# A decoder trunk in split float32: gate/up and key/value products by one level of Strassen

## The chip, the cores and the metric

The kernel runs on one core of one Trainium2 chip. The metric is the device time of one execution in microseconds, as the median of several runs. The kernel before takes 2006.05 us (three runs, 2004.75 to 2006.26).

The core's engines work side by side, each through its own instructions in order: TensorE (PE) multiplies, VectorE (DVE) and ScalarE (ACT) work on elements, GpSimd (POOL) adds and issues some transfers, SyncE (SP) issues most transfers. PE writes to PSUM, which has eight banks of 128 partitions x 512 float32.

## The reference

Sixteen learned meta tokens stand ahead of 512 tokens, 528 in all, with 1024 features. Two layers follow. The first mixes tokens by a short gated convolution, the second by forgetting attention over eight heads, whose keys and values are computed once, between the layers. Each layer has a feed-forward before and one behind the mixer:

```python
def swiglu(x, wg, wu, wd):
    return (jax.nn.silu(x @ wg) * (x @ wu)) @ wd
...
h = layer_norm(DEEPNORM_ALPHA * h + 0.5 * swiglu(h, ffn1_wg[l], ffn1_wu[l], ffn1_wd[l]), ...)
mix = short_conv(...) if l < N_A else forgetting_attention(h, ..., k_sh, v_sh, c_sh)
h = layer_norm(DEEPNORM_ALPHA * h + mix, ...)
h = layer_norm(DEEPNORM_ALPHA * h + 0.5 * swiglu(h, ffn2_wg[l], ffn2_wu[l], ffn2_wd[l]), ...)
if l == N_A - 1:
    k_sh, v_sh, c_sh = shared_kv(h, kv_w, f_bias)
```

The hidden width is 2816 (22 tiles of 128). The gates of the attention are eight further columns of `kv_w`. All is float32, and the meta tokens are dropped from the output.

## The kernel before, in words

Activations lie with features on partitions: `y` is 128 x 8 tiles x 528 tokens. A float32 number is kept as two parts of the type float32r, which PE multiplies in one pass: the cast (`xh`, `wh`, on ACT) and what it leaves (`xl`, `wl`, a subtract on DVE). A product is then three matmuls for each of the eight tiles k of the contraction, wl·xh, wh·xl and wh·xh (`gemms`, line 164). Weights are loaded two 128-column tiles at a time, 1 MB, into `rawp` (line 99) and split one tile of 8 x 128 columns at a time (`split_w`, lines 109 and 110) into one of eight pairs of buffers (`wp`).

Tokens are worked in two parts, the halves: 272 and 256 columns in layer 0, 256 and 256 in layer 1, where the meta columns drop out. Layer 1 has a third part that is both halves at once, 512 columns, one PSUM bank. It is used wherever no norm is near.

A feed-forward (`ffn`) runs over its 22 hidden tiles in chunks of 6, 8 and 8. For each tile and half, `unit` multiplies gate and up side by side, then `finish` takes silu on ACT (line 317), multiplies on DVE (318) and splits the result into `hh` and `hl` (181, 182). At the end of a chunk `down` contracts over the chunk's tiles and adds into `y` (293). In the last chunk the layer norm follows, and the order there is: tiles 0 to 2 of half 0, of half 1, tiles 3 to 7 of half 0, of half 1.

The norm (`Norm`) works by halves. `pre` shifts all by about the mean once tile 0 is there (219 or 223). `add` squares each finished tile on ACT and adds the tile and its square into two running sums on POOL (236, 238). `post` turns the sums into statistics by two float32 matmuls (244, 245), takes 1/sqrt in eight dependent DVE operations (187 to 195), and then, tile by tile, scales and shifts (257, 258 on DVE, 260 on ACT) and splits (181, 182). PE's order is that of the program text, so `post` is put behind some of the products that follow, by `later(n, fn)`: `fn` is written behind n further tiles of contraction. `LAG = (6, 20)` is n for half 0 and half 1. For half 0 these are products of half 1 of the same matrix. For half 1 they are the next stage's first products, which `lagged` puts in order so that three hidden tiles (or two of the convolution's, or six heads) do half 0 before any does half 1.

The other engines' order is made by a planner: on each engine the earliest instruction of the program text among those that its model has ready.

Of the kernel before, what the change touches and what calls it, by code (L numbers as in the profile page):

```python
# [9 lines left out]
F32 = mybir.dt.float32  # L10
# [12 lines left out]
M = 16  # L23
# [20 lines left out]
def trunk_kernel(  # L44
# [10 lines left out]
    hid = ctx.enter_context(tc.tile_pool(name="hid", bufs=8))  # L55
    rawp = ctx.enter_context(tc.tile_pool(name="rawp", bufs=2))
    wp = ctx.enter_context(tc.tile_pool(name="wp", bufs=8))
    dram = ctx.enter_context(tc.tile_pool(name="dram", bufs=1, space=DRAM))
    nrm = ctx.enter_context(tc.tile_pool(name="nrm", bufs=1))
# [21 lines left out]
    c_keep = cpool.tile([H, T], F32, name="c_keep")  # L81

# [1 line left out]
    y = act.tile([P, KD, T], F32, name="y")  # L84
    xh = act.tile([P, KD, T], F32R, name="xh")
    xl = act.tile([P, KD, T], F32R, name="xl")
# [10 lines left out]
    def load_raw(w_ap, r0, kn, c0, cn):  # L97
        raw = rawp.tile([P, KD, 256], F32, tag="raw", name="raw")
        nc.sync.dma_start(
            raw[:, :kn, :cn],  # L100
            w_ap[r0:r0 + kn * P, c0:c0 + cn].rearrange("(k p) n -> p k n", p=P),
        )
        return raw

    def split_w(raw, kn, c0):
        wh = wp.tile([P, KD, P], F32R, tag="wh", name="wh")
        wl = wp.tile([P, KD, P], F32R, tag="wl", name="wl")
        src = raw[:, :kn, c0:c0 + P]
        nc.scalar.copy(wh[:, :kn, :], src)  # L109
        nc.vector.tensor_tensor(  # L110
            wl[:, :kn, :], src, wh[:, :kn, :].bitcast(F32), ALU.subtract
        )
        return wh, wl

    class Weights:
        """m-tiles of one matrix's block, loaded two at a time and split when first used; with
        `lead`, the first is loaded alone."""

        def __init__(self, w_ap, r0, kn, c0, n, lead=False):
            self.a, self.r0, self.kn, self.c0, self.n = w_ap, r0, kn, c0, n  # L120
            cuts = [0] + ([1] if lead else []) + list(range(3 if lead else 2, n, 2)) + [n]
            self.block = {m: (a, b) for a, b in zip(cuts, cuts[1:]) for m in range(a, b)}
            self.raw, self.got = {}, {}

        def load(self, m):
            a, b = self.block[m]
            if a not in self.raw:
                self.raw[a] = load_raw(
                    self.a, self.r0, self.kn, self.c0 + a * P, (b - a) * P)
            return a, b  # L130

        def __call__(self, m):
            if m not in self.got:
                a, b = self.load(m)
                for j in range(a, b):
                    self.got[j] = split_w(self.raw[a], self.kn, (j - a) * P)
            return self.got[m]

# [19 lines left out]
    def gemms(jobs, ks, start=True, stop=True):  # L158
        """For each (ps, w, (rh, rl)): ps (+)= w.T @ (rh + rl) over the tiles ks of the
        contraction, side by side."""  # L160
        for k in ks:
            for ps, (wh, wl), (rh, rl) in jobs:
                for j, (a, b) in enumerate(((wl, rh), (wh, rl), (wh, rh))):
                    nc.tensor.matmul(  # L164
                        ps, lhsT=a[:, k, :], rhs=b(k),
                        start=start and k == ks[0] and j == 0,
                        stop=stop and k == ks[-1] and j == 2)
# [7 lines left out]

    def x_operands(h, layer):
        a, b = cols(xh, h, layer), cols(xl, h, layer)
        return (lambda k: a[:, k, :]), (lambda k: b[:, k, :])
# [4 lines left out]

    def rsqrt(v, r, a):
        """r = 1 / sqrt(v), v and a spent: a guess from the exponent, Newton's step, kept as
        r = 3/8 of it, and a step of third order, (15 - 10 e + 3 e^2) / 8 with e = v (8/3 r)^2."""
# [11 lines left out]
    class Norm:  # L198
        def __init__(self, layer, i, eps):
            self.layer, self.i, self.eps = layer, i, eps  # L200
            self.s1, self.s2 = {}, {}

        def tmp(self, h, tag, bufs=2):
            w = SPAN[self.layer][h][1]
            return nrm.tile([P, 272], F32, tag=tag, bufs=bufs, name=tag)[:, :w]

        def pre(self, h, scale):
            """With the first tile complete: shift all by about its mean, the others scaled first."""
            yv = cols(y, h, self.layer)
            w = yv.shape[2]  # L210
            first = nrm.tile([P, 272], F32R, tag="first", bufs=1, name="first")[:, :w]
            nc.scalar.copy(first, yv[:, 0, :])

            def shift():
# [11 lines left out]
                nc.scalar.activation(self.s2[h], yv[:, 0, :], AF.Square)  # L226

            later(6, shift)

        def add(self, h, m):  # L230
            yv = cols(y, h, self.layer)
# [8 lines left out]
        def post(self, h):  # L240
# [5 lines left out]
            d2 = self.tmp(h, "d2", 1)  # L246
            nc.scalar.activation(d2, pd, AF.Square)
            v = self.tmp(h, "v", 1)
            nc.vector.scalar_tensor_tensor(v, pv, self.eps, d2, ALU.add, ALU.subtract)
            r, a = self.tmp(h, "r"), self.tmp(h, "a", 1)  # L250
            rsqrt(v, r, a)
            b = self.tmp(h, "b")
            nc.vector.scalar_tensor_tensor(b, pd, -1.0, r, ALU.mult, ALU.mult)
            xhv, xlv = cols(xh, h, self.layer), cols(xl, h, self.layer)
            for m in range(KD):
                ym = yv[:, m, :]
                nc.vector.tensor_tensor(ym, ym, r, ALU.mult)  # L257
                nc.vector.tensor_tensor(ym, ym, b, ALU.add)  # L258
                c = self.i * KD + m
                nc.scalar.activation(  # L260
                    ym, ym, AF.Identity, scale=vecs[:, c:c + 1], bias=vecs[:, 48 + c:49 + c])
                split_x(xhv[:, m, :], xlv[:, m, :], ym)
# [494 lines left out]
```

## Time and profile before

| | before |
|---|---|
| median of three runs | 2006.05 us (2004.75 to 2006.26) |
| span of the profiled execution | 2004.3 us |
| instructions | 31831 |
| matmuls | 13783 |
| busy: PE, DVE, ACT, POOL | 1973.8, 913.0, 632.5, 146.6 us |
| read from HBM | 181.76 MB, 94 GB/s over the span |

The span is what the trace covers of one execution, 1.75 us less than the median. Busy time of PE runs to a matmul's modelled end, and matmuls overlap: one of 256 columns is shown with 281 ns though the next begins 118 ns later. So the pitch, from start to start, is read where many stand in a row. DVE's operations overlap by some 0.08 us in the same way.

### The profile page before, as it was taken

How to read it: one execution, taken by the hardware profiler on the slowest of the kernel's cores; microseconds unless marked ns; L12 is line 12 of the kernel's file. 1: busy time of each engine (PE TensorE's matmuls, PEld its weight loads, DVE VectorE, ACT ScalarE, POOL GpSimd, SP SyncE). 2: the span in 40 equal slices, each digit the busy share in tenths (PEclk: the TensorE clock that was granted, in tenths of full speed). 3: DMA queues.
4: the chain of work that ended last, by engine and by line, in shares of the span. 5: the costliest groups of instructions: out<-in, count | busy, mean ns of one | idle time of the engine just before them, and what ended most of it. 6: DMA issues, size and time to landing. Idle time of an engine off the chain costs nothing.

```text
span 2004.3 us, 31831 instructions
## 1 busy us (share of the span) xinstructions
PE 1973.8 (98%) x13783; PEld 1842.2 (92%) x13783; DVE 913.0 (46%) x1558; ACT 632.5 (32%) x1114; POOL 146.6 (7%) x216
## 2 busy tenths in 40 slices
PE   8999999999999999999999999999999999999997
PEld 8999999989999999999999988888998898888887
DVE  5333333574467433333655242333388683333334
ACT  4222222353235222122442222212255452222220
POOL 0000000410040000000411000000220310000000
PEclk9999999999999999999999999999999999999999
DMA  6233223122222332233243233232323223323211
GB/s 202 85 100 101 85 85 105 64 79 91 85 85 90 101 105 85 86 101 89 64 149 119 74 110 101 87 103 85 112 90 114 91 68 122 105 88 101 89 59 43
DMA packets 180332, 190.25 MB, mean 95 GB/s; under 512 B 3980, under 2 KB 174264, under 8 KB 180192
## 3 DMA queue, kind: packets, MB, share of 16 engines
q1 hardware_dynamic: 178176, 182.73, 28.1%
q0 software_dynamic: 2016, 5.49, 0.8%
q8 instruction: 108, 1.77, 0.4%
q14 instruction: 32, 0.26, 0.0%
HBM read 181.76 MB, written 6.44 MB: 94 GB/s over the span
## 4 chain that ended last, share of the span: by engine, by line
PE 93%; DVE 5%; POOL 1%; issue 1%; DMA 0%; ACT 0%; POOLq 0%; SPq 0%; DVEq 0%
PE pg L164 25%; PE pu L164 25%; PE pv L164 2%; PE pcb L164 2%; PE pcc L164 2%; PE pcv L164 2%; PE pk L164 2%; PE pq L164 2%; DVE y L257 1%; PE psc L569 1%; DVE wl L110 1%; PE po L617 1%; DVE y L258 1%; POOL s L236 1%; DVE xl L182 0%
## 5 line engine op out<-in xcount | busy, mean ns | idle before, releaser
L110 DVE TENSOR_TENSOR wl<-raw,wh 128x1024 fp32r<-128x1024 f32 (+1 forms) x336 | 407.8, 1226 | 116.1 <-ACT wh L109 114.1
L109 ACT CAST wh<-raw 128x1024 fp32r<-128x1024 f32 (+1 forms) x336 | 339.7, 1027 | 303.8 <-DMA raw<-in_ffn_wg_dram 7.7
L164 PE MATMUL pg<-xh,wl 128*128 128x256 f32 (+2 forms) x1120 | 350.1, 313 | 1.5 <-ACT xh L181 1.5
L164 PE MATMUL pg<-xl,wh 128*128 128x256 f32 (+2 forms) x1120 | 350.9, 313 | 0.5 <-DVE xl L182 0.5
L164 PE MATMUL pg<-xh,wh 128*128 128x256 f32 (+2 forms) x1120 | 349.4, 312 | 0.0
L164 PE MATMUL pu<-xl,wh 128*128 128x256 f32 (+2 forms) x1120 | 348.6, 311 | 0.0
L164 PE MATMUL pu<-xh,wl 128*128 128x256 f32 (+2 forms) x1120 | 348.5, 311 | 0.0
L164 PE MATMUL pu<-xh,wh 128*128 128x256 f32 (+2 forms) x1120 | 348.1, 311 | 0.0
L318 DVE TENSOR_TENSOR sg<-sg,pu 128x256 f32<-128x256 f32 (+2 forms) x140 | 69.2, 495 | 583.6 <-ACT sg L317 313.1
L317 ACT ACTIVATE sg<-pg 128x256 f32<-128x256 f32 (+2 forms) x140 | 62.0, 443 | 669.3 <-PE pg L164 669.3
L164 PEld LDWEIGHTS pg<-xh,wl 128*128 128x128 f32 x1120 | 211.5, 189 | 14.3 <-ACT xh L181 1.9
L164 PEld LDWEIGHTS pu<-xh,wl 128*128 128x128 f32 x1120 | 210.7, 188 | 13.7
L164 PEld LDWEIGHTS pg<-xh,wh 128*128 128x128 f32 x1120 | 211.5, 189 | 12.6
L164 PEld LDWEIGHTS pg<-xl,wh 128*128 128x128 f32 x1120 | 211.1, 188 | 13.0 <-DVE xl L182 0.9
L164 PEld LDWEIGHTS pu<-xh,wh 128*128 128x128 f32 x1120 | 210.4, 188 | 12.8
L164 PEld LDWEIGHTS pu<-xl,wh 128*128 128x128 f32 x1120 | 210.3, 188 | 12.7
L182 DVE TENSOR_TENSOR hl<-sg,hh 128x256 fp32r<-128x256 f32 (+2 forms) x140 | 69.2, 495 | 22.5 <-ACT hh L181 22.4
L181 ACT CAST hh<-sg 128x256 fp32r<-128x256 f32 (+2 forms) x140 | 65.0, 465 | 27.6 <-DVE sg L318 27.6
L236 POOL TENSOR_TENSOR s<-s,y 128x256 f32<-128x256 f32 (+1 forms) x60 | 59.0, 983 | 90.9 <-DVE y L293 90.2
L236 POOL TENSOR_TENSOR s<-y 128x256 f32<-128x256 f32 (+1 forms) x10 | 7.5, 751 | 784.0 <-DVE y L293 784.0
L238 POOL TENSOR_TENSOR s<-s,sq 128x256 f32<-128x256 f32 (+1 forms) x70 | 58.9, 843 | 0.9
L260 ACT ACTIVATE y<-y,vecs 128x256 f32<-128x256 f32 (+1 forms) x80 | 45.1, 599 | 25.6 <-DVE y L258 25.4
(1516 smaller groups left out, 3994.6 us busy)
## 6 DMA issues: line engine op xcount, KB each, us to landing
raw<-in_ffn_wg_dram SPq DMA_DIRECT2D x43, 1024.0 KB, 5.2
raw<-in_ffn_wu_dram SPq DMA_DIRECT2D x43, 1024.0 KB, 5.2
raw<-in_ffn_wd_dram SPq DMA_DIRECT2D x32, 1024.0 KB, 5.1
raw<-in_ffn_wd_dram SPq DMA_DIRECT2D x16, 768.0 KB, 4.5
raw<-in_conv_w_in_dram SPq DMA_DIRECT2D x12, 1024.0 KB, 5.1
raw<-in_kv_w_dram SPq DMA_DIRECT2D x8, 1024.0 KB, 5.7
raw<-in_conv_w_out_dram SPq DMA_DIRECT2D x4, 1024.0 KB, 5.1
raw<-in_attn_w_q_dram SPq DMA_DIRECT2D x4, 1024.0 KB, 5.3
```

What stands on the lines that cost most here:

```text
L109: nc.scalar.copy(wh[:, :kn, :], src)
L110: nc.vector.tensor_tensor(wl[:, :kn, :], src, wh[:, :kn, :].bitcast(F32), ALU.subtract)
L164: nc.tensor.matmul(ps, lhsT=a[:, k, :], rhs=b(k), start=start and k == ks[0] and j == 0, stop=stop and k == ks[-1] and j == 2)
L181: nc.scalar.copy(dst_h, src32)
L182: nc.vector.tensor_tensor(dst_l, src32, dst_h.bitcast(F32), ALU.subtract)
L236: nc.gpsimd.tensor_tensor(self.s1[h], yv[:, 0, :] if m == 1 else self.s1[h], yv[:, m, :], ALU.add)
L238: nc.gpsimd.tensor_tensor(self.s2[h], self.s2[h], sq, ALU.add)
L257: nc.vector.tensor_tensor(ym, ym, r, ALU.mult)
L258: nc.vector.tensor_tensor(ym, ym, b, ALU.add)
L260: nc.scalar.activation(ym, ym, AF.Identity, scale=vecs[:, c:c + 1], bias=vecs[:, 48 + c:49 + c])
L317: nc.scalar.activation(sg, pg, AF.Silu)
L318: nc.vector.tensor_tensor(sg, sg, pu, ALU.mult)
```

## The change

In each feed-forward, gate and up are multiplied 256 columns of hidden features at a time, as a 2 x 2 matrix of blocks times a 2 x 2 matrix of blocks: the weight's quarters a11 to a22 are 128 features x 512 of the contraction, the operand's quarters b11 to b22 are 512 features x one half of the tokens. Strassen's algorithm in Winograd's form makes the four blocks of the result from seven products of sums of quarters. Keys and values are done the same way, with the key's columns in the place of the gate's.

- `Quads` loads a unit's weights in two raw buffers (one for each half of the contraction, for both matrices), makes four sums s1 to s4 on DVE, in place but for s1, and splits seven parts of 1024 columns.
- `Mixed` holds the seven operands, and `made` makes them from `y` when a pair of tiles is normed: n11 = -b11 and b21 for half 0, and, with half 1, t1 = b11 - b12, t3 = b12 - b22, t2 = b11 - t3, t4 = b21 - t2, b22, each split. `Plain` holds ordinary operands, for the convolution and the queries.
- `Unit` has the seven products. Three of them add onto another's PSUM bank. In between, ACT and DVE carry partial results to SBUF.
- `run_units` gives their order. `Norm.post` now works on two tiles at a time, in the order 0, 4, 2, 6.
- Chunks are 6, 6, 6 and 4 tiles. Both halves of layer 0 are 264 columns. The first feed-forward of layer 1 uses the operands of the keys and values, 264 wide.
- Tile pools that were opened stage by stage become shared ones: `wp` has five pairs where it had eight, `rawp` three buffers where it had two, `xp` 14, `hid` 12, `gup` 8.

```diff
-CHUNKS = ((0, 6), (6, 8), (14, 8))
+CHUNKS = ((0, 6), (6, 6), (12, 6), (18, 4))
-SPAN = (((0, 272), (272, 256)), ((16, 256), (272, 256), (16, 512)))
+SPAN = (((0, 264), (264, 264)), ((16, 256), (272, 256), (16, 512)))
...
+    class Quads:
...
+        def sums(self):
...
+            nc.vector.tensor_tensor(s, a21, a22, ALU.add)
+            nc.vector.tensor_tensor(a21, a11, a21, ALU.add)
+            nc.vector.tensor_tensor(a11, a11, s, ALU.add)
...
+    class Mixed:
...
+        def made(self, h, m):
...
+            if h == 0 and m < KH:
+                a, c = self.tiles("n11", k)
+                nc.scalar.mul(a, b(0, 0), -1.0)
+                nc.vector.scalar_tensor_tensor(
+                    c, b(0, 0), -1.0, a.bitcast(F32), ALU.mult, ALU.subtract)
+            elif h == 0:
+                split_x(*self.tiles("b21", k), b(1, 0))
+            self.done.add((h, m))
+            if h == 0 or not {(1, k), (1, k + KH)} <= self.done:
+                return
...
+            sub(t1, b(0, 0), b(0, 1))
+            split_x(*self.tiles("t1", k), t1)
+            sub(t3, b(0, 1), b(1, 1))
+            sub(t2, b(0, 0), t3)
+            split_x(*self.tiles("t2", k), t2)
+            split_x(*self.tiles("t3", k), t3)
+            t4 = new("t4")
+            sub(t4, b(1, 0), t2)
+            split_x(*self.tiles("t4", k), t4)
+            split_x(*self.tiles("b22", k), b(1, 1))
...
-            for m in range(KD):
-                ym = yv[:, m, :]
-                nc.vector.tensor_tensor(ym, ym, r, ALU.mult)
-                nc.vector.tensor_tensor(ym, ym, b, ALU.add)
...
+            for m in (0, KH, 2, KH + 2):
+                ym = yv[:, m:m + 2, :]
+                nc.vector.tensor_tensor(ym, ym, rb, ALU.mult)
+                nc.vector.tensor_tensor(ym, ym, bb, ALU.add)
+                for j in range(m, m + 2):
...
+                self.to.made(h, m)
...
+        def product(self, bank, left, right, start):
+            if start:
+                self.bank(bank)
+            wh, wl = self.quads(left)
+            for j in range(2):
+                gemms([(self.t[bank][j], (wh[:, j], wl[:, j]), self.xs[right])], range(KH),
+                      start=start, chained=True)
...
+        def p1(self):
+            self.product("b", "a11", "n11", True)
+            for j in range(2):
+                nc.scalar.copy(self.out(j, 0, 0), self.t["b"][j])
...
+        def p2(self):
+            self.product("a", "a12", "b21", True)
+            for j in range(2):
+                o = self.out(j, 0, 0)
+                nc.vector.tensor_tensor(o, self.t["a"][j], o, ALU.subtract)
...
+        def p5(self):
+            self.product("c", "s1", "t1", True)
...
+        def p6(self):
+            self.product("b", "s2", "t2", False)
+            for j in range(2):
+                nc.scalar.copy(self.out(j, 0, 1), self.t["b"][j])
...
+        def p7(self):
+            self.product("b", "s3", "t3", False)
+            for j in range(2):
+                o = self.out(j, 1, 1)
+                nc.scalar.copy(o, self.t["b"][j])
+                nc.vector.tensor_tensor(o, o, self.t["c"][j], ALU.subtract)
...
+        def p4(self):
+            self.product("b", "a22", "t4", False)
...
+        def p3(self):
+            self.product("c", "s4", "b22", False)
+            for j in range(2):
+                o = self.out(j, 0, 1)
+                nc.vector.tensor_tensor(o, self.t["c"][j], o, ALU.subtract)
...
+    def run_units(units, finish, after=None):
+        units[0].p1()
+        units[0].p2()
+        for i, u in enumerate(units):
+            nxt = units[i + 1] if i + 1 < len(units) else None
+            if i == 0 and nxt:
+                nxt.p1()
+            u.p5()
+            u.p6()
+            if i == 0 or not nxt:
+                u.p7()
+            else:
+                u.p7()
+                nxt.p1()
+            u.p4()
+            u.p3()
+            finish(i, u)
...
+            if nxt:
+                nxt.p2()
...
+            def finish(i, u, hh=hh, hl=hl):
...
+                for m in (1, 0):
...
+                        nc.scalar.activation(g[0][:, :2 * w], g[0][:, :2 * w], AF.Silu)
+                        nc.vector.tensor_tensor(
+                            g[0][:, :2 * w], g[0][:, :2 * w], v[0][:, :2 * w], ALU.mult)
+                    split_x(hh[j][:, o0:o0 + 2 * w], hl[j][:, o0:o0 + 2 * w], g[m][:, :2 * w])
```

Before the first unit of the program all of x is transposed (`turn_x(0)`, `turn_x(1)`), where half 1 stood behind eight tiles of contraction. The convolution's first two tiles do `us` (two products) of half 0 for both, and one gate product, before half 1; the queries do five heads of half 0 first, then three of half 1.

## Rows read from the trace of the kernel before

**Rows 1.** The page, part 1: busy us (share of the span) xinstructions of each engine

```profile
PE 1973.8 (98%) x13783; PEld 1842.2 (92%) x13783; DVE 913.0 (46%) x1558; ACT 632.5 (32%) x1114; POOL 146.6 (7%) x216
```

**Rows 2.** The page, part 4: the chain that ended last, by engine, by line

```profile
PE 93%; DVE 5%; POOL 1%; issue 1%; DMA 0%; ACT 0%; POOLq 0%; SPq 0%; DVEq 0%
PE pg L164 25%; PE pu L164 25%; PE pv L164 2%; PE pcb L164 2%; PE pcc L164 2%; PE pcv L164 2%; PE pk L164 2%; PE pq L164 2%; DVE y L257 1%; PE psc L569 1%; DVE wl L110 1%; PE po L617 1%; DVE y L258 1%; POOL s L236 1%; DVE xl L182 0%
```

**Rows 3.** Waits of PE: us in total, times, longest us

```profile
PE pd L244 <- POOL s L236: 3.1, 1, 3.1
PE pv L245 <- POOL s L238: 3.0, 4, 1.1
...
PE pk L164 <- ACT xh L181: 0.9, 1, 0.9
```

**Rows 4.** The chain in order of time: start us, us, what

```profile
219.98 3.02 PE pd__2351 L164 x24
223.00 2.84 PE pd__2377 L164 x24
...
1055.00 5.87 PE pv L164 x48
...
1293.16 5.55 PE pd__13163 L164 x24
```

**Rows 5.** Groups of PE by form: busy us, mean ns of one, idle before

```profile
L164 PE MATMUL pg<-xh,wl 128*128 128x256 f32 x480 | 135.1, 281 | 0.6 <-ACT xh L181 0.6
...
L164 PE MATMUL pg<-xl,wh 128*128 128x512 f32 x288 | 114.5, 398 | 0.0
...
L164 PE MATMUL pg<-xl,wh 128*128 128x272 f32 x352 | 102.5, 291 | 0.3 <-DVE xl L182 0.3
```

**Rows 6.** Groups of DVE by form

```profile
L110 DVE TENSOR_TENSOR wl<-raw,wh 128x1024 fp32r<-128x1024 f32 x304 | 377.9, 1255 | 109.2 <-ACT wh L109 107.2 <-DMA vt<-v_dram 0.7
...
L318 DVE TENSOR_TENSOR sg<-sg,pu 128x512 f32<-128x512 f32 x36 | 24.8, 688 | 270.5 <-PE pu L164 270.5
```

**Rows 7.** DVE in order of time: start us, us, engine line op out<-in xcount

```profile
408.73 1.22 DVE L110 TENSOR_TENSOR wl<-raw,wh 128x1024 fp32r<-128x1024 f32 x1
409.87 0.79 DVE L182 TENSOR_TENSOR xl<-y,xh 128x272 fp32r<-128x272 f32 x2
410.57 2.36 DVE L110 TENSOR_TENSOR wl<-raw,wh 128x1024 fp32r<-128x1024 f32 x2
```

**Rows 8.** Groups of ACT by form

```profile
L109 ACT CAST wh<-raw 128x1024 fp32r<-128x1024 f32 x304 | 314.0, 1048 | 300.3 <-DMA raw<-in_ffn_wg_dram 7.7 <-issue 5.7 <-PE pd__8923 L164 4.9
...
L181 ACT CAST hh<-sg 128x512 fp32r<-128x512 f32 x36 | 22.2, 618 | 0.0
```

**Rows 9.** DVE in order of time, norm ahead of the keys, half 1

```profile
1001.85 0.41 DVE L249 SCALAR_TENSOR_TENSOR v<-pv,d 128x256 f32<-128x256 f32 x1
...
1006.18 0.75 DVE L257 TENSOR_TENSOR y<-y,r 128x256 f32<-128x256 f32 x2
...
1008.86 0.76 DVE L182 TENSOR_TENSOR xl<-y,xh 128x256 fp32r<-128x256 f32 x2
```

**Rows 10.** Groups of POOL by form

```profile
L238 POOL TENSOR_TENSOR s<-s,sq 128x272 f32<-128x272 f32 x21 | 16.2, 769 | 0.0
```

**Rows 11.** Stretches: us, busy us (x) by engine, PEclk, DMA share, GB/s

```profile
414.30:418.90 4.60, 3.76 (x14) 3.18 (x15) 1.14 (x3) 0.77 (x2) 1.41 (x3) 0.64 0.71 231
418.90:425.00 6.10, 6.10 (x50) 6.10 (x50) 5.73 (x16) 1.14 (x3) 0.00 (x0) 0.99 0.00 0
...
416.50:418.90 2.40, 2.40 (x12) 2.31 (x11) 1.14 (x3) 0.39 (x1) 0.00 (x0) 0.50 0.43 143
```

**Rows 12.** PE in order of time, the first product

```profile
12.48 0.57 PE L164 MATMUL pg<-xh,wl 128*128 128x272 f32 x1
```

**Rows 13.** The page, part 6: DMA issues, median us to landing

```profile
raw<-in_ffn_wg_dram SPq DMA_DIRECT2D x43, 1024.0 KB, 5.2
```

**Rows 14.** The chain from 405 to 415 us

```profile
408.99 4.52 POOL s L236
```

More of the change, by code (lines that the diff above doesn't have):

```diff
@@ L336, in operands @@
                 return (lambda k: hh[k][:, o:o + w]), (lambda k: hl[k][:, o:o + w])
+            wts = Weights(wd, f0 * P, fn, 0, KD)
             if last and c == len(CHUNKS) - 1:
[L339 removed]
+                last(wts, fn, operands)
                 return
[L341 removed]
+            down(layer, wts, fn, operands, c == 0,
                  norm if c == len(CHUNKS) - 1 else None, 2 * ALPHA)
@@ new lines, in trunk_kernel @@
+    half = D // 2
+    rows = ((0, P), (P, 120), (248, P), (376, P), (504, 8))
+    mt = [htile("mt", F32)[:M, :half] for _ in range(2)]
+    for j in range(2):
+        nc.sync.dma_start(mt[j], meta[:, j * half:(j + 1) * half])
+    xt = []
+    for r0, n in rows:
+        xt.append([htile("xt", F32)[:n, :half] for _ in range(2)])
+        for j in range(2):
+            nc.sync.dma_start(xt[-1][j], x[0, r0:r0 + n, j * half:(j + 1) * half])
+    vr = gtile("vr", P)[:120]
+    nc.gpsimd.dma_start(vr[0:48, :], ln_gain.rearrange("l i (m p) -> (l i m) p", p=P))
@@ new lines, in turn_x, with turn_vecs, ztile @@
+            xs0.made(h, m0)
+    def turn_vecs():
+        ps = psum("pvec")
+        nc.tensor.transpose(out=ps[:, :120], in_=vr, identity=ident[:120, :120])
+        nc.vector.tensor_copy(vecs, ps[:, :120])
+    turn_x(0)
+    turn_x(1)
+    later(8 * KD, turn_vecs)
+    xc = Plain(0)
+    ffn(0, ffn1_wg[0], ffn1_wu[0], ffn1_wd[0], 0, xs0, xc)
+    w_in = [Weights(conv_w_in[0], 0, KD, j * D, KD) for j in range(3)]
+    zh, zl = {}, {}
+    us = {}
+    def ztile(d, i, name):
+        if i not in d:
+            if i < 6:
+                d[i] = htile(name)
+            else:
+                t = xtile(name).rearrange("p k c -> p (k c)")
+                d[6], d[7] = t[:, :T], t[:, T:2 * T]
+        return d[i]
@@ new lines, in trunk_kernel, with z_operands @@
+    for part, i, h in (
+            (conv_u, 0, 0), (conv_u, 1, 0), (conv_b, 0, 0), (conv_u, 0, 1), (conv_b, 0, 1),
+            (conv_u, 1, 1), (conv_b, 1, 0), (conv_b, 1, 1)):
+        run([part(i, h)])
+    for i in range(2, KD):
+        for h in range(2):
+            run([conv_u(i, h), conv_b(i, h)])
+    def z_operands(h):
+        o, w = SPAN[0][h]
+        return (lambda k: zh[k][:, o:o + w]), (lambda k: zl[k][:, o:o + w])
+    xs1 = Mixed(0)
+    down(0, Weights(conv_w_out[0], 0, KD, 0, KD), KD, z_operands, True,
+         Norm(0, 1, EPS, xs1), ALPHA)
@@ L461, in trunk_kernel, with kv_done, gates @@
+    def kv_done(i, u):
+        for j in range(2):
+            nc.scalar.copy(u.out(j, 1, 0), u.t["b"][j])
+        for m in range(2):
+            head = 2 * i + m
+            nc.gpsimd.dma_start(k_dram[head], u.t[0, m])
+            later(KD, lambda head=head, vT=u.t[1, m]: turn_v(head, vT))
+    c_keep = nrm.tile([H, T], F32, name="c_keep")
+    def gates(i):
+        if i != 1:
+            return
+        fr = tiny.tile([P, KD, H], F32, tag="fr", bufs=1, name="fr")
         nc.gpsimd.dma_start(fr, kv_w[:, 2 * D:2 * D + H].rearrange("(k p) n -> p k n", p=P))
-        fh = wp.tile([P, KD, P], F32R, tag="wh", name="fh")
@@ new lines, in trunk_kernel @@
+    fetch(0)
+    project(range(3), [0])
+    project(range(3, 5), [0])
+    project(range(3), [1])
+    q_w(5)
+    step(0)
+    for head in range(3, 7):
+        project([head], [1] if head < 5 else [0, 1])
+        if head < 6:
+            step(head - 2)
+    for m in range(AHEAD):
+        o_w(m)
+    step(4)
+    project([7], [0, 1])
+    step(5)
+    ahead(range(3))
+    step(6)
+    ahead([3])
+    step(7)
+    ahead([4])
+    turn(6)
+    ahead([5])
+    mix(6)
+    turn(7)
+    ahead([6])
@@ L728 @@
+    ffn(1, ffn2_wg[1], ffn2_wu[1], ffn2_wd[1], 5, xs3, None, last=last)
 _INS = [
```

770 lines of the change are left out of this document (402 added, 368 removed).

## The prediction, made before the changed kernel was built or run

> **What bounds the kernel now.** The page's list of engines comes first: PE is busy for 1973.8 of 2004.3 us, DVE for 913.0 [rows 1]. The chain that ended last is PE for 93%, half of it the gate and up products [rows 2]. A busy PE could still be a waiting one, so the waits come next: the longest wait that is not at the start is 3.1 us, for a POOL sum ahead of a layer norm's statistics [rows 3]. The chain in order of time then gives the rate: 24 matmuls take 5.55 us at 512 columns (231.2 ns each), 3.02 at 272, 2.84 at 256 (118.3 ns), and 48 of the two halves together 5.87, or 122.2 ns for one of 264 on the mean [rows 4]. So the kernel is bound by the number of matmul columns, and all else is hidden behind them. The profiled span is 2004.3 us, 1.75 below the median of the runs (2006.05); the sum is made in span and 1.75 added.
>
> **Fewer products.** In a feed-forward of layer 0 the gate and up products are 2 x 22 x 8 x 3 x 2 halves = 2112 matmuls (352 of 272 columns in each of six forms are those of both [rows 5]), 258.1 us at 122.2 ns. Afterwards they are 11 units x 7 products x 2 matrices x 4 k x 3 parts = 1848 of 264 columns: 225.8. That is -32.3, twice: -64.6. In layer 1 the old form is 864 of 512 columns and 384 of 256, 245.2 us. Its first feed-forward takes over the operands made for keys and values, 264 wide with the meta columns: 225.8, or -19.4. The last is 256 wide: 218.6, or -26.6. Keys and values: 768 become 672 matmuls, -11.7; the gates' product grows from 48 to 60, +1.5. The last chunk with four tiles instead of eight leaves 96 contraction steps per pass to the 512-wide form: -1.0 in both passes. Together **-121.8 us**, and since PE has no other slack, this is taken off the path in full, if PE is fed.
>
> The Trainium skill, in "TensorE: Matmul & The Clock Gate" (section "Wait — 56ns, not 53.3ns?"), puts a warm matmul at its columns over 2.4 GHz and about 2.5 ns; that would make one of 264 columns 112.5 ns and the saving, an estimate, about 116 us. The trace has 122.2 ns, so the measurement decides.
>
> **What feeds a unit.** A unit is 168 matmuls, 20.5 us. DVE subtracts seven weight parts of 1024 columns where it had four, and adds four sums of that size. One takes 1255 ns on the mean, but one in a row of them takes 1.22 us and two take 2.36, so the pitch is 1.14 [rows 6, 7]; on the same line 264 columns cost 0.35 and 528 0.62. Eleven of the first (12.5), eight of 264 (2.8) and three of 528 (1.9) make 17.2 us of 20.5. ACT has seven casts of 1048 ns at most [rows 8] and some 4 us else, 12. Both fit, and five weight buffers let the parts run four products (11.7 us) ahead. Taken as 0; the other end is 0.4 us in each of 48 units, 20, if evictions queue behind 1.14 us operations.
>
> **Ends of chunks.** The unit's last product, p3, is followed by a chain before the down product can use its two hidden tiles: subtract from PSUM 0.4, multiply by the up part 0.69, cast 0.62, subtract 0.69 [rows 6, 8], some 2.8 us with 0.1 between them. Before, the last tile came eighth in the contraction, after 7 x 0.37 = 2.6 us. Now it is tile 4 of 6 (1.5 us, wait 1.3) or 2 of 4 (0.7 us, wait 2.0). At 512 columns four tiles cover 2.8 us: nothing. With six chunks of the first kind and four of the second 16 us; ends 10 and 24 (DVE in one more 1.14 us operation each time). I take **+16**.
>
> **Layer norms into mixed operands** (three: before the second feed-forward, the keys, the last). The second half's statistics are still issued 20 contraction steps behind the last product, but the half-0 work in front of them is now three products, 24 steps of 0.37: PE has 1.5 us left when the sums go out. Product p5 needs t1 = half 0 minus half 1, so the whole chain of the second half: from the variance to the first scaling 4.3 us (1001.85 to 1006.18), to the first subtract of the split 2.7 more [rows 9]. Now pairs 0 and 4 are both scaled (528 columns, one further ACT pass of about 1.0), then t1 subtracted, cast and split (2.0): 11 us, 9.5 beyond PE's cover. The third pair waits behind the nine other operations that `made` writes for the first two (9 x 0.62), so the third k tile is 6 us later still unless DVE's order brings it forward: 15.5. Ends 9.5 and 18; I take 13, nearer to 15.5: **+39**. What stands behind p5 (t2, t3, t4) is ready by then.
>
> **Order of pairs** (all five norms): the half-0 tiles come as pairs 0, 4, 2, 6, but a product contracts 0, 1, 2, 3. Pair 2 is some 3 us behind pair 0 where 0.7 to 1.5 us are covered: 0 to 2.5 each, taken at 1.5: **+7.5**.
>
> **Last chunk of four tiles** (three norms). A down product ahead of the norm is 12 matmuls, 1.47 us, where it was 24 and 2.9. Each is followed by two POOL additions of 0.77 us [rows 10], 1.54: POOL falls behind, and the first half's statistics, which PE issues in order ahead of the remaining products, wait for it. Those products, 5 x 1.47 = 7.3 us, are also all that covers the first half's own chain of 8 us or more; they were 14.7, and PE still waited 0.9 us for xh [rows 3]. Ends 3 (POOL alone, free) and 15 (below, rival 2); I take 8: **+24**. Earlier additions than these are not on the path.
>
> **The clock.** After PE's wait of 3.1 us [rows 3], which ended at 414.3, the granted clock was 0.64 until 418.9 on the mean, 0.50 (1.2 GHz) in its second half and 0.99 (2.4 GHz) from then on [rows 11]: 0.36 x 4.6 = 1.7 us. Waits above 3 us now come in two to eight places; five: **+8.5** (ends 3 and 14).
>
> **The rest.** At the start all rows of x are transposed before the first product, and DVE makes 22 operands of 528 columns (13.6 us) beside the first weights; before, the first product began at 12.48 with half of x [rows 12]. Ends 2 and 14, **+6**. Into the convolution and the queries the half-0 cover falls from 144 to 120 matmuls, 2.9 us: ends 0 and 8, **+4**. The waits for POOL at second halves go, since the statistics go out later: **-6** of 6.1 [rows 3]. Pools: raw weights have three buffers for two halves per unit, 1 MB each with 5.2 us to land [rows 13], used up in 20.5; nothing.
>
> **Sum.** -121.8 + 16 + 39 + 7.5 + 24 + 8.5 + 6 + 4 - 6 = -22.8: span 1981.5, time **1983**. With all low ends 1931, with all high ends 2070.
>
> **Rivals.**
> 1. *The cover holds.* DVE's order favours what PE waits for, the norms cost as little as now (under 1 us at most places [rows 3]), and only chunk ends and start are left: -122 + 12 - 6, 1890. For it: DVE is idle more than half the time [rows 1]. Against it: the 4.3 us of dependent operations are no matter of order. Chance 0.14, 1890 to 1935.
> 2. *DVE and POOL shut each other out around the norms, and it is slower.* While DVE ran its subtractions without a gap from 408.73 to 412.9, a POOL addition that takes 0.77 us elsewhere took 4.52 [rows 7, 10, 14]. In the down product of a four-tile chunk (23.5 us) POOL has 28 additions, 21 us, and DVE some 16 us with two SBUF inputs, sums and parts of the next weights among them: 37. Then each of these three norms costs 15, the mixed ones 18 in the second half and 2.5 in order, and the start 10: -122 + 45 + 54 + 12.5 + 12 + 20 + 10 + 4 - 6, 2032. It decides from where all waits together pass 122 us. Against it: additions whose DVE neighbour reads PSUM run at 0.77, and a DVE that waits for PE leaves gaps. Chance 0.24, 2005 to 2060.
> 3. *DVE bounds the units.* At 17.2 of 20.5 us, 20% of stretch is enough; at 1 us in each of 48 units +48, 2031. Against it: sums and splits for the first unit of a chunk lie in the down product, where DVE has 20 us free. Chance 0.08.
>
> The Trainium skill, in "SBUF — State Buffer" (section "SBUF: two separate sides"), has a port pair that DVE and GpSimd lock for one whole instruction, the loser waiting until it ends. By that an addition would wait for one subtraction, 1.2 us at most, and rival 2's norms would cost nearer 8 than 15, some 21 us less in all. The row of 4.52 us does not agree, and I follow the row.
>
> **How the numbers follow.** The forecast has 0.54 and by itself 1940 to 2002. 0.2%, 4 us, is what a measurement can tell from no change: 2002 to 2010. Forecast: 0.52 faster, 0.02 same; rival 1: 0.14 faster; rival 2: 0.03 same, 0.21 slower; rival 3: 0.03 same, 0.05 slower. Faster 0.66, same 0.08, slower 0.26. The range that leaves out 2 in 10 runs from 1925 to 2040.
>
> **What would show it.** 8064 matmuls of 256 and 264 columns in gate, up, keys and values at 118 to 122 ns; in PE's waits, p5's first matmul behind the split of t1, 9 to 16 us at three places; the statistics of first halves behind POOL, 2 to 8 us at three; the first down products behind hl, 1 to 2 us at ten; PE without waits inside a chunk. It is wrong if PE waits inside units by more than 20 us in all, or if the p5 waits are under 5 us.

## The result: 2068 us, 3.1% slower

The changed kernel takes 2068.43 us (2064.16 to 2069.41), the kernel before on the same chip 2006.15: a ratio of 1.0306, with a 95% interval of 1.0291 to 1.0321. The forecast was 1983, faster. The profiled execution has a span of 2066.2 us. Here are the engines' busy times and the shares of the chain that ended last, both from the page of the profile, to be read against [rows 1, 2]:

```profile
PE 1899.9 (92%) x14235; PEld 1821.2 (88%) x14235; DVE 1449.8 (70%) x2112; ACT 893.1 (43%) x1472; POOL 153.7 (7%) x218
...
PE 82%; DVE 12%; issue 2%; ACT 2%; DMA 2%; POOL 1%; SPq 0%; DVEq 0%; ACTq 0%; POOLq 0%
```

PE is idle for 166 us of the span where it was idle for 30, and DVE's share of the chain rises from 5% to 12%. Inside the products nothing has changed. In the chain in order of time, 24 matmuls of 264 columns take 2.92 us, 121.7 ns each, where [rows 4] had 125.8 for 272 columns and 118.3 for 256:

```profile
706.56 2.92 PE pc L225 x24
```

Counted at its pitch, each width's matmuls come to 1763.7 us where they were 1885.4. That is -121.7, the first term of the forecast (0.4 ns less in the pitch of 264 columns, which the trace does not exclude, would make it -125.6). What ate the saving is in the waits of PE (us in total, times, longest), which answer to [rows 3]:

```profile
PE pc L225 <- ACT xh L238: 48.4, 6, 12.7
PE pb L225 <- ACT xh L287: 19.0, 6, 9.2
PE pcc L225 <- ACT xh L238: 12.9, 3, 11.3
PE pb L225 <- DVE wl L118: 11.0, 1, 11.0
PE pq L225 <- ACT xh L238: 10.5, 2, 9.1
PE pd L379 <- POOL s L371: 8.6, 3, 3.6
PE pcb L225 <- DVE wl L118: 6.3, 5, 1.3
```

The first line is p5 behind the three mixed norms, each time one wait of 12 and one of 4 us. The second, third and fifth are for the most part first halves, whose normed tiles come late; the sixth is their sums on POOL. The fourth is the start, the seventh the convolution. The waits between products, counted from start to start less the pitch, are 161 us where they were 15.5 (the start comes on top), and matmuls below full clock cost 27.3 us instead of 5.5.

The stretch behind a norm shows why. It runs from the first half's statistics to the first matmul that needs the second half, which is p5 in the changed kernel. Two answers of the view by stretches follow (us, then busy us of PE, PEld, DVE, ACT and POOL, PEclk, DMA share, GB/s): the changed kernel ahead of its second feed-forward, and the kernel before from the same statistics to its first matmul on half 1.

```profile
602.40:647.60 45.20, 27.05 (x184) 25.46 (x182) 41.40 (x60) 19.98 (x34) 11.74 (x11) 0.80 0.15 47
```

```profile
585.70:620.75 35.05, 32.84 (x256) 31.79 (x255) 33.41 (x69) 18.80 (x39) 10.08 (x11) 1.00 0.28 91
```

DVE was busy for 33.4 of 35.05 us there before the change as well, under an average of 46%: the stretch had 1.6 us to spare. The change moves both sides. DVE is now busy for 41.4 us there, 8 more, and PE has 184 matmuls (22 us at their pitch) to cover it, where it had 256 (31 us).

### The profile page after: what moved, and what is told of

It reads as the page before. It is cut to its first block, busy times and chain, and to the rows that moved or that the text cites. A ratio compares the mean times of both kernels' runs of the same rounds, so it can differ in the third digit from the quotient of the medians.

```text
span 2066.2 us, 34226 instructions
## 1 busy us (share of the span) xinstructions
PE 1899.9 (92%) x14235; PEld 1821.2 (88%) x14235; DVE 1449.8 (70%) x2112; ACT 893.1 (43%) x1472; POOL 153.7 (7%) x218
## 4 chain that ended last, share of the span: by engine, by line
PE 82%; DVE 12%; issue 2%; ACT 2%; DMA 2%; POOL 1%; SPq 0%; DVEq 0%; ACTq 0%; POOLq 0%
PE pb L225 26%; PE pc L225 13%; PE pa L225 6%; DVE wl L118 3%; PE pcc L225 2%; PE pcb L225 2%; PE pcv L225 2%; PE pq L225 2%; DVE y L391 1%; DVE xl L239 1%; DVE y L392 1%; PE psc L817 1%; DMA raw<-in_kv_w_dram 1%; PE po L875 1%; ACT wh L117 1%
## 5 line engine op out<-in xcount | busy, mean ns | idle before, releaser
L225 PE MATMUL pb<-xh,wl 128*128 128x264 f32 (+1 forms) x1536 | 440.2, 287 | 30.6 <-ACT xh L287 19.0
L225 PE MATMUL pb<-xl,wh 128*128 128x264 f32 (+1 forms) x1536 | 438.8, 286 | 4.5 <-DVE xl L288 4.5
L225 PE MATMUL pb<-xh,wh 128*128 128x264 f32 (+1 forms) x1536 | 438.8, 286 | 0.0
L225 PEld LDWEIGHTS pb<-xh,wl 128*128 128x128 f32 x1536 | 292.9, 191 | 33.2 <-ACT xh L287 20.6
L225 PEld LDWEIGHTS pb<-xl,wh 128*128 128x128 f32 x1536 | 292.8, 191 | 6.6 <-DVE xl L288 6.2
L225 PEld LDWEIGHTS pb<-xh,wh 128*128 128x128 f32 x1536 | 293.1, 191 | 0.0
L225 PE MATMUL pc<-xh,wl 128*128 128x264 f32 (+1 forms) x768 | 221.5, 288 | 49.7 <-ACT xh L238 48.4
L225 PE MATMUL pc<-xl,wh 128*128 128x264 f32 (+1 forms) x768 | 221.1, 288 | 4.0 <-DVE xl L239 4.0
L225 PE MATMUL pc<-xh,wh 128*128 128x264 f32 (+1 forms) x768 | 220.6, 287 | 0.0
L225 PEld LDWEIGHTS pc<-xh,wh 128*128 128x128 f32 x768 | 147.8, 192 | 0.0
```

What stands on the lines that cost most here:

```text
L225: nc.tensor.matmul(ps, lhsT=a[:, k, :], rhs=b(k), start=start and k == ks[0] and j == 0, stop=stop and k == ks[-1] and j == 2, skip_group_ ...
```

## The experiments

All times are medians, beside the changed kernel's 2068.4 and 2006 for the kernel before. The texts on what was expected name four theories. T: chains of dependent operations have too little cover. D: DVE has more work around a norm than the stretch is long. L: DVE and POOL shut each other out. O: the order of DVE's operations is at fault. First came single parts of the norms.

**Chunks.** The chunk ahead of a norm gets six tiles again.

```diff
+FIRST4 = ((0, 4), (4, 6), (10, 6), (16, 6))
...
-        for c, (f0, fn) in enumerate(CHUNKS):
+        for c, (f0, fn) in enumerate(CHUNKS if last else FIRST4):
```

> The three feed-forwards that end in a norm take chunks of 4, 6, 6, 6 tiles, so the chunk ahead of the norm has six tiles again (the last feed-forward keeps 6, 6, 6, 4). Theory T (a four-tile product of 1.47 us covers too little, and POOL's two additions of 0.75 outrun it): the three waits for POOL (3.3 us each) go, the five products behind the first half's statistics cover 11 us and not 7.3, so the waits for xh of 10 to 12 us fall by 3.7 each; with the low clock behind them -21 to -28 us, 2040 to 2047. Rival L (DVE and POOL shut each other out at every norm): more time per addition ends the jam altogether, -40 or more, below 2030. If neither cover nor jam matters: 2063 to 2073.

The time is 2058.0, -10: a miss. The waits for POOL at the three places shrink to one of 0.5 us, but those for xh behind them are 7.9, 11.1 and 9.7 us (11.5, 9.4 and 9.2 before the edit): only one falls. Now 6.6 to 10.2 us of weight parts and of sums from PSUM stand between the steps of the first half's 1/sqrt (4.6 to 5.2 before the edit), so DVE fills the longer cover.

**Additions on DVE.**

```diff
-            nc.gpsimd.tensor_tensor(
+            nc.vector.tensor_tensor(
                 self.s1[h], yv[:, 0, :] if m == 1 else self.s1[h], yv[:, m, :], ALU.add)
-            nc.gpsimd.tensor_tensor(self.s2[h], self.s2[h], sq, ALU.add)
+            nc.vector.tensor_tensor(self.s2[h], self.s2[h], sq, ALU.add)
```

> The norms' running sums are added on DVE instead of POOL. Theory T (dependent chains and too little cover; POOL is late at first halves only): about 10 us of waits for POOL go, DVE gets 14 x 0.35 us more for each half, so -10 to +5 us, 2058 to 2073. Rival L (POOL and DVE shut each other out, so that both are slow around the norms): -40 us or more, below 2030.

The time is 2029.5, -39: theory L's size, to within 1 us. The engines and PE's waits in this run:

```profile
PE 1889.4 (93%) x14235; PEld 1813.3 (89%) x14235; DVE 1467.7 (72%) x2252; ACT 891.9 (44%) x1472; POOL 25.6 (1%) x78
```

```profile
PE pc L225 <- ACT xh L238: 45.7, 6, 12.2
...
PE pb L225 <- ACT xh L287: 10.0, 6, 6.3
PE pcc L225 <- ACT xh L238: 8.1, 3, 6.3
PE pq L225 <- ACT xh L238: 7.6, 2, 6.2
```

DVE takes over 140 additions of some 0.42 us, 59 us, and its busy time rises by 17.9 only. Some 14 us of the difference is overlap with their neighbours. The rest is DVE's other operations, which take 27.5 us less in all than in the changed kernel: by so much had POOL's additions stretched them. The stretch shown in the result is 6 us shorter in this run, with 36.7 us of DVE in it and not 41.4:

```profile
594.90:634.00 39.10, 25.54 (x185) 24.24 (x183) 36.66 (x67) 20.36 (x35) 0.00 (x0) 0.85 0.17 55
```

The changed kernel's trace shows one place of such stretching, POOL first, then DVE:

```profile
586.91 1.77 POOL L371 TENSOR_TENSOR s<-s,y 128x264 f32<-128x264 f32 x1
...
592.05 0.75 POOL L371 TENSOR_TENSOR s<-s,y 128x264 f32<-128x264 f32 x1
```

```profile
586.85 1.23 DVE L118 TENSOR_TENSOR wl<-raw,wh 128x1024 fp32r<-128x1024 f32 x1 [0.51 <-ACT wh L117]
587.99 1.77 DVE L182 TENSOR_TENSOR s<-raw 128x1024 f32<-128x1024 f32 x1
```

Beside DVE's long operations an addition of 0.75 us takes 1.77, and one of DVE's operations of 1.22 us takes 1.77 too. The Trainium skill, in "SBUF — State Buffer" (section "SBUF: two separate sides"), has whichever starts first keep the shared ports for its whole instruction; 1.0 us lost beside operations of 1.2 agrees with that here, better than the 4.52 of [rows 14] did. Such stretching is not new with the change. Take DVE's operations that last over 1.15 times the median of their shape, and add up what they last beyond that median: 28 us in the kernel before, 31 in the changed one, 6 in this run. In this run it is the first halves that gain most; p5 still waits 45.7 us.

**Order of pairs.**

```diff
-            for m in (0, KH, 2, KH + 2):
+            for m in range(0, KD, 2):
...
+            if m < KH:
+                t1 = new("t1")
+                sub(t1, b(0, 0), b(0, 1))
+                split_x(*self.tiles("t1", k), t1)
+                return
```

> The norm works its pairs of tiles in the order 0, 2, 4, 6, and t1 (which needs only tiles 0 to 3 of both halves) is made before t3, t2, t4 and b22. Theory T (p5 waits for a dependent chain in which t1's second pair stands behind nine other operations): the second waits of 4.2 and 1.3 us at three places go, the first ones lose a pair's scaling (about 2 us each), and the waits for the second pair at five first halves (7.8 in all) go: -25 to -31 us, 2037 to 2044. Rival D (DVE's amount of work at the norms is what bounds): p6 and p7 wait for what p5 no longer waits for, and the time stays within 5 us of 2068.

The time is 2053.2, -15: between the two theories. The second waits of 4.2 us go, but the first are still 13.0, 12.1 and 13.1 us, and p6 now waits up to 1.8.

**Statistics earlier.**

```diff
-LAG = (6, 20)
+LAG = (6, 6)
```

> The second half's statistics are written 6 contraction steps behind the last product instead of 20, for all five norms. POOL's sums were ready 6.4 to 15.7 us before PE asked for them. Theory T: the chain begins 14 x 0.366 = 5.1 us earlier, the three first waits of 12 us ahead of p5 fall by as much, with the clock -15 to -18 us, 2050 to 2053. Rival D (DVE is full with the first half's scaling and the weight parts then): the chain is only stretched, less than 5 us.

The time is 2037.2, -31, more than theory T had. PE's first waits ahead of p5 fall from 12 to 5 us each:

```profile
PE pc L225 <- ACT xh L238: 26.2, 6, 5.0
```

An earlier start gains more than its 5.1 us. In the changed kernel DVE is idle for 2.3 of the 6 us ahead of the old place (628 to 634) and full behind it. In this run two weight parts and not four stand between the steps of 1/sqrt, which then takes 6.6 to 7.5 us and not 8.6 to 9.5.

**No dependence on the second half.** `Mixed(layer, solo=True)` reads half 0 in the place of half 1 for all seven operands.

> Behind the three norms that make mixed operands, all seven are made from half 0 alone (another result), so p5 does not depend on the second half's statistics. It prices the p5 waits with the low clock behind them. Theory T (the long dependent chain of the second half is what PE waits for): 57 us of waits and some 8 of low clock go, -60 to -66, 2002 to 2008. Theory D (DVE has more work around a norm than the stretch is long: it is busy for 36.4 of 39 us from 616 to 655): PE then waits for the weight parts or for t2 and t3 instead, and only 20 to 40 us are gained, 2028 to 2048.

The time is 2039.8, -29: theory D. With the dependence taken away altogether, half the gain that theory T expected of it is there. PE waits for POOL's sums (15.1 us, 8.6 in the changed kernel) and for weight parts instead:

```profile
PE pd L382 <- POOL s L374: 15.1, 5, 3.5
...
PE pc L225 <- DVE wl L118: 6.2, 2, 3.1
```

**Weight parts.** Two tries at the same parts: `u.quads("s1"); u.quads("s2")` written ahead of `nxt.p1()`, and the four sums left out.

> The first unit's weight parts s1 and s2 (three sums and two splits) are written ahead of the second unit's p1, and so ahead of the second half's statistics in the text. In the trace four such operations of 1.22 us stand between the dependent steps of 1/sqrt and make 4.4 us to 8.6 or 9.1. Theory O (DVE's order is at fault): 4.9 us less at three places, with the clock -14 to -18, 2050 to 2054. Theory D (DVE is full there in any order): the operations take the time of others, less than 5 us.

The time is 2072.5, +4. The edit did not do what it was to: four operations of the same kind still stand in each chain, three of them sums of the second unit, which are ready early and not needed for a unit's time. So this run says nothing on either theory.

> The four sums of quarters are left out of every unit (another result): 4.6 us less of DVE in each 20.5 us unit, nothing else changed. Theory D (around a norm DVE is the bound, and the weight parts of the next units are part of it): the waits at the norms fall by 2 to 4 us at eight or more places, -20 to -35 with the clock, 2033 to 2048. If DVE's load is not the bound, but only the length of the dependent chain without the sums: -0 to -8.

The time is 2046.0, -22, in theory D's range. The engines in this run:

```profile
PE 1896.9 (93%) x14235; PEld 1820.6 (89%) x14235; DVE 1235.0 (60%) x1920; ACT 893.4 (44%) x1472; POOL 146.3 (7%) x218
```

DVE has 215 us less work, and a tenth of that reaches the time, at the norms: p5's first waits are 9.1, 8.9 and 8.8 us. The sums that went were also among the parts between the steps of 1/sqrt (one part is left there of four), so this run alone does not tell load from order.

**Small edits.**

```diff
-            run([conv_u(i, h), conv_b(i, h)])
+        for part in (conv_u, conv_b):
+            for h in range(2):
+                run([part(i, h)])
...
-    turn_x(1)
...
+            gemms([(pair[m, h], w(m), operands(h)) for m, h in pair], range(kn))
```

> Three small edits at separate places. Convolution: both halves of u, then both of b, from tile 2 on (five waits of 1.43 for a weight part, 7 us). Chunk ends: the first down products are contracted side by side, four at a time, or two ahead of a norm (six ends at 1.4 us, three at 2.7: 16 us). Start: the transposes of the second half of x stand behind p1 and p2 of the first unit (11 us of wait for the first weight part). If each wait goes without a successor: -30 to -34 us, 2034 to 2038. If each is only moved (to the next product, to p5 at the start): -5 to -15.

The convolution now does u of both halves and then b, `turn_x(1)` stands behind p1 and p2 of the first unit, and the first down products of a chunk are contracted side by side. The time is 2050.4, -18, between the two expectations. The convolution's five waits go. The first product begins at 17 us and not 32, but p5 of the first two units then waits 3.9 and 2.7. Ends of six tiles are free of waits; the three ahead of a norm keep 2.0 of 2.7 us, and the norm's first matmul waits up to 2.0 behind them.

**The clock.** Matmuls whose sum is not used, where PE waits.

```diff
+                    for n in range(96):
+                        nc.tensor.matmul(
+                            junk, lhsT=wh[:, n % 2, n // 2 % KH, :], rhs=u.xs["n11"][0](n // 2 % KH),
+                            start=n == 0, stop=n == 95)
```

> 96 further matmuls of 264 columns (11.7 us, their sum is not used) stand ahead of the first p5 behind each mixed norm, where PE otherwise waits 12 us. The waits stay; the granted clock should not fall. If the clock's loss there is real: -5 to -9 us, 2059 to 2063. If the stretch behind the wait is bound by DVE and not by PE's clock: within 2 us of 2068.

The time is 2175.8. The matmuls stood at the first unit of each of the thirteen chunks that use these three norms' operands, so ten times 11.7 us were added where PE had no such wait, and the run decides nothing. At the three places alone:

> 96 further matmuls of 264 columns (11.7 us, their sum is not used) ahead of the first p5 behind each of the three mixed norms alone, where PE otherwise waits 12 us. If the low clock behind these waits is a cost of its own: -6 to -10, 2058 to 2062. If what follows is bound by DVE anyway: within 3 us of 2068.

The time is 2061.6, -6.9: the low clock is a cost of its own, 2.3 us at each place on the mean. In the changed kernel PE had waited 12 us, and the stretch behind that wait ran at half clock (1.2 GHz), as the first line shows. In this run, the second line, 633 to 650 stays at full clock (2.4 GHz), where the changed kernel has 0.69; from 650 to 665, behind the second wait, it is 0.77 against 0.66.

```profile
647.60:655.20 7.60, 2.64 (x7) 1.73 (x7) 7.60 (x14) 5.88 (x12) 0.00 (x0) 0.50 0.00 0
```

```profile
633.00:650.00 17.00, 15.43 (x123) 15.08 (x122) 16.18 (x27) 7.65 (x14) 0.00 (x0) 1.00 0.20 63
```

**Order or load.** All weight parts that the text has behind a norm's statistics are held on DVE until `b`, the last of the dependent steps, is there:

```diff
-        nc.vector.tensor_tensor(b, src, a.bitcast(F32), ALU.subtract)
+        with behind_chain():
+            nc.vector.tensor_tensor(b, src, a.bitcast(F32), ALU.subtract)
```

> Every weight part (sum or split) that the text has behind a norm's statistics is held back on DVE until the last of the dependent steps; no other edit. In the trace of the changed kernel 4.9 us of such parts, sums for the second unit among them, stand between the steps at three second halves, 3 to 6.5 us at five first halves. Theory O (the order is at fault): 4.9 x 3 and some 2 to 5 us at each first half less, with the clock -25 to -35, 2033 to 2043. Theory D (DVE is full there in any order): the parts are only later, p5 or p6 wait for them, within 6 us of 2068.

The time is 2074.1, +6, in theory D's range. DVE in order of time, first in the changed kernel, then in this run:

```profile
636.86 0.43 DVE L322 SCALAR_TENSOR_TENSOR a<-r 128x264 f32<-128x264 f32 x1
637.26 1.23 DVE L182 TENSOR_TENSOR s<-raw 128x1024 f32<-128x1024 f32 x1
638.40 0.43 DVE L323 TENSOR_TENSOR v<-v,a 128x264 f32<-128x264 f32 x1
638.75 1.22 DVE L118 TENSOR_TENSOR wl<-raw,wh 128x1024 fp32r<-128x1024 f32 x1
639.88 0.43 DVE L324 SCALAR_TENSOR_TENSOR a<-v 128x264 f32<-128x264 f32 x1
640.23 1.22 DVE L183 TENSOR_TENSOR raw<-raw 128x1024 f32<-128x1024 f32 x1
641.36 0.43 DVE L325 SCALAR_TENSOR_TENSOR r<-a,r 128x264 f32<-128x264 f32 x1
641.70 1.22 DVE L184 TENSOR_TENSOR raw<-raw,s 128x1024 f32<-128x1024 f32 x1
642.84 0.43 DVE L387 SCALAR_TENSOR_TENSOR b<-pd,r 128x264 f32<-128x264 f32 x1
```

```profile
630.78 0.43 DVE L391 SCALAR_TENSOR_TENSOR v<-pv,v 128x264 f32<-128x264 f32 x1 [1.91 <-PE pv L388]
...
634.85 0.43 DVE L395 SCALAR_TENSOR_TENSOR b<-pd,r 128x264 f32<-128x264 f32 x1
...
650.69 0.69 DVE L247 TENSOR_TENSOR xl<-t,xh 128x528 fp32r<-128x528 f32 x1
651.31 1.21 DVE L188 TENSOR_TENSOR s<-raw 128x1024 f32<-128x1024 f32 x1
...
653.70 1.22 DVE L124 TENSOR_TENSOR wl<-s,wh 128x1024 fp32r<-128x1024 f32 x1
```

The chain is as short as in the kernel before, 4.5 us. Then the operands' work runs without a gap to 651, and p5's own weight part, which was held as well, comes behind it. So p5 waits longer than ever, for that part:

```profile
PE pc L233 <- DVE wl L124: 68.1, 3, 22.8
```

**Together.** The edits for additions, order, statistics and small places; the same with additions on POOL; the first with six-tile chunks.

> Four of the edits together: additions on DVE, pairs in the order 0, 2, 4, 6 with t1 first, statistics of the second half 6 steps behind, and the three small edits. Alone they gave -39, -15, -31 and -18. If they take away different waits: 1965. If DVE's work around the norms is what remains (theory D), they share the gain: 1980 to 2000. In both cases faster than the kernel before, 2006.

The time is 2002.1: the gains of -39, -15, -31 and -18 are shared (-66, not -103), as theory D has it, if 2 us above its range.

> The same without the additions' move: they stay on POOL. If the gains add: 2004. The difference from the run with the additions on DVE is what POOL costs when nothing else is left in front of it: 25 to 40 us by the single runs; under 10 if the order alone had been what POOL disturbed.

The time is 2021.7, so POOL costs 19.5 us here, below the 25 to 40 of the single runs.

> The four edits and chunks of 4, 6, 6, 6 tiles ahead of a norm. The chunks alone gave -10. If the cover of the first half's chain is still what is missing: 8 to 15 us below the run of the four edits; if additions on DVE already closed that gap: within 4 us of it.

The time is 1998.2, 3.9 below the run of the four edits, at the edge: there is little left for a longer cover to close.

On top of that run, the hold on all parts, with two lags:

> The same hold on top of the run with the four edits and chunks of 4, 6, 6, 6 (1998). There 7.3 to 8.2 us of weight parts stand in the chains of the three second halves, and PE waits 8.7 to 9.6 us ahead of p5. Theory O: -15 to -24, 1974 to 1983. Theory D: within 6 us of 1998, with waits for weight parts in the place of those for t1.

> As f2_all_gate with the second half's statistics 12 steps behind the last product and not 6: DVE's sums, for which PE waits 2 us at two places, have 2.2 us more. If the hold delays the parts that p2 and the second unit's p1 need, this is 3 to 8 us faster than f2_all_gate; if the chain's start is what counts, 4 to 7 us slower.

The times are 2045.1 and 2047.5: both far slower, outside what either theory gave. In the first, p2 waits up to 13.8 us for its part at three places; in the second, the next unit's p1 up to 13.2. A hold on all parts, then, delays what PE needs next, here and in the run before, and does not tell whether an order that respects need would help. So last, only the parts that are needed late are held, without and with extra matmuls:

> On the run with the four edits and chunks of 4, 6, 6, 6 (1998): only the parts that are needed late are held behind the dependent steps: s3, a22 and s4 of the first unit, all but a11 of the next ones. Three of the six parts of 1.22 us in each of three chains go. Theory D with an order that respects need: 3.7 us less at three places, and what was held is made in p5's and p6's time, -8 to -14 with the clock, 1984 to 1990. If DVE is full to the last: p6 and p7 wait for what p5 gains, within 5 us of 1998.

The time is 1996.1, 2 below the run without the hold and within the 5 us of a DVE that is full to the last. The first line is the wait in the run without the hold, the next ones this run's:

```profile
PE pc L226 <- ACT xh L239: 27.0, 3, 9.6
```

```profile
PE pc L234 <- ACT xh L247: 13.9, 3, 6.5
PE pc L234 <- DVE wl L121: 8.9, 3, 3.4
...
PE pb L234 <- DVE wl L121: 5.7, 2, 3.4
```

Of 13.1 us less in the wait for xh, 7.9 come back in the two for weight parts, which were 3.3 and 3.4 without the hold and are 8.9 and 5.7 with it.

> As g1_hold, with 48 further matmuls (5.9 us, their sum is not used) ahead of the first p5 at the three places, in the time in which PE waits anyway. If the low clock costs what it did alone (about 2.3 us at each place): -4 to -7 against g1_hold. If the wait is already shorter than 5.9 us: slower than g1_hold.

The time is 1995.1, 1 below, which is within the noise, where -4 to -7 was expected. Both are faster than the kernel before: 0.9943, interval 0.9926 to 0.9959. So the seven products win 0.6% in another arrangement, not the 6% of their matmuls (the kernel before was not given the same edits).

## Why the prediction was wrong

| term | forecast | measured |
|---|---|---|
| matmuls | -121.8 | -121.7 |
| mixed norms, second half | +39 | +56.6 (18.5, 19.0, 19.1) |
| four-tile last chunk | +24 | +42.9 |
| clock | +8.5 | +21.8 |
| start | +6 | +19.1 |
| chunk ends | +16 | +19.2 |
| order of pairs | +7.5 | +7.8 |
| conv/query cover; POOL waits | +4; -6 | +6; -6 |
| weight parts of the convolution; first halves behind eight tiles | 0 | +7; +7 |

The right side adds up to +60, the spans differ by 61.9. Measured means the waits of PE at that place, start to start less the pitch, less what stood there before the change.

**Right:** the saving, the waits' places, the order of pairs and PE without waits inside a chunk. Six of the ten chunk ends wait 1.4 us, where 1.3 was worked out, and four wait 2.7, where 2.0 was. Of the signs that the prediction named, only these four ends lie outside.

**Wrong in size: the load on DVE behind a norm.** The step that failed is in "What feeds a unit". It set DVE's 17.2 of 20.5 us per unit against whole units, said "Both fit" and took 0. The chains behind the norms were then priced as if DVE did nothing else: 1/sqrt from a chain of 4.3 us [rows 9]. The two were never added for the same stretch. Behind a norm DVE has to do both, and is busy for 41.4 us until p5, against 22 us of matmuls. From the variance to the first scaling it took 8.5 us and not 4.3, since four weight parts, 4.9 us, stand between the steps. So p5's first wait was 12 to 13 us where 9.5 was worked out. The third pair came 6 us later, as worked out; but the forecast took 13 and not its own 15.5, in the hope that DVE's order would bring that pair forward, which it did not. That makes the 18.5 to 19.1.

**How far the runs show this.** With the dependence of p5 on the second half taken away, half the gain expected of it is there, and PE waits for POOL and DVE instead. With the sums left out the time falls by 22, with the statistics earlier, where DVE has gaps, by 31. An order by need in the full stretch gives 2 us in the last arrangement, and 15 in the changed kernel. The hold on all parts proves less than it seems to: the chain is short without the weight parts, and p5 is later because its own part was held too. It is the hold on late parts alone, whose gain at p5 comes back as waits for weight parts, that speaks against the order as the cause.

**The four-tile chunk** has a second cause. Of its 43 us, 18 go when the additions leave POOL, waits for POOL's sums among them, and 7 of the first halves behind eight tiles with them. With six tiles, DVE's work fills the longer cover. **The start and the convolution** are other matters. At the start the first weight part comes behind 22 operand operations on DVE, and PE waits 11 us for it. In the convolution PE waits for a weight part five times, though DVE is busy for only 7.8 us of each 19; another order of the products ends these waits. The clock's 21.8 us lie behind the waits.

**The ends.** The sum with all high ends was 2070, and the time came within 2 us of it, but by luck. 20 us of that sum are DVE's stretch of the units, which did not come. Without them it is 2050. Norms (56.6 against 54), clock (21.8 against 14) and start (19.1 against 14) went beyond their high ends, and 14 us came where 0 had been set. Norms, last chunk and clock had been taken at or below the middle of their ranges, as if they could miss either way, but a DVE without room pushes all of them up at once.

**Rival 2** had the sign and nearly the prices: 15 and 18 us per norm, 14.3 and 18.9 measured. Its mechanism, DVE and POOL shutting each other out, is worth at most 39 us of the 85 by which the forecast missed, by the run with additions on DVE. The 18 at mixed norms came out by luck: p5 waits 45.7 us of its 48.4 with POOL out of the way. The terms of its sum add up to 2035.5, not 2032. It fell short of 2068 at the start (10 against 19.1) and by the 14 us that no term had; two of its terms, 12 and 20, have no name and can't be compared one by one. **Rival 3** asked for 1 us in each of 48 units. DVE does bound, but at the norms only.

What stays open: how much of the 39 us is the stretching of DVE's operations (27.5 us), how much POOL's own lag, and how much the order that the move brings; and whether a list of DVE's operations written out for need could do better than 1995, which was not tried.

## What to carry to other kernels

An engine that is busy 46% on the mean can be 95% busy at the one place where a change adds work. So before pricing a dependent chain from a stretch where the engine was free, add up its work for each stage, old and new, and the matmuls that cover it, old and new: here the work rose by 8 us and the cover fell by 9. When several costs hang on the same full engine, their high ends come together. A product saved on one engine is worth what the next one can take.

## What the runs showed of the hardware

- An addition on POOL is not free for DVE: 140 additions of 0.75 us made DVE's other operations 27.5 us longer in all. With the additions on DVE its busy time rose by 17.9 us, and the kernel gained 39.
- A wait of 12 us on PE cost some 2.3 us more behind it, at half clock (1.2 GHz); matmuls in the wait whose sum is not used gave that back (-6.9 us at three places).
